# Row maxima as one VectorE scan, and VectorE's and ScalarE's order written out through the four value and gate blocks of the mLSTM layer

## The chip, the cores and the metric

The kernel runs on one core of one Trainium2 chip. The metric is the device time of one execution in microseconds (us). Before the change three runs took 598.82, 599.16 and 599.52 us, median 599.16 us.

## The reference, cut to what matters

The model has two layers over 256 positions of width 1024: an mLSTM mixer with a convolutional feed-forward network, then block-sparse attention with a second such network. The change touches the mixer alone. For each of its 4 heads (128 wide for q and k, 256 wide for v), with gates i and f:

```
u = rmsnorm(x) @ w_in ;  q, k, v, o, i, f = split(u)
b_t  = cumsum(log_sigmoid(f))                      # per head, over time
m_t  = b_t + max(0, max over s<=t of (i_s - b_s))  # "row maximum"
S_ts = (q_t . k_s) / sqrt(128) * exp(b_t - b_s + i_s - m_t)    for s <= t
h_t  = sum_s S_ts v_s / max(|sum_s S_ts|, exp(-m_t))
out  = (rmsnorm(h) * sigmoid(o)) @ w_out ;  x += out
```

The reference walks over chunks of 64 positions; the kernel does all 256 at once, which is the same sum. The running maximum over s is the part that the change computes in another way.

## The kernel before, in words

All matmuls are done on operands split in two: `hi`, a rounded copy that ScalarE makes, and `lo`, the remainder that VectorE makes; three products (hi.x, lo.x, hi.x_lo) give the needed precision. A weight arrives by DMA in units of 128x2048 numbers. `unit` takes a raw buffer (3 of them), has SyncE load it, and splits it in two pieces of 1024 columns: ScalarE `hi` (L144), VectorE `lo` (L145). There are 4 buffers for `hi` and 4 for `lo`.

**Order of the work.** TensorE runs in program order in the whole kernel (`manual_schedule`). VectorE and ScalarE run in program order from the start to `first.close()` (L579); behind that a planner places their instructions by its own estimates, and it may put a planned instruction ahead of a written one. GpSimd and SyncE are planned throughout. `behind(marks, ...)` makes the planner queue some instructions behind others. `mix(steps, items)` interleaves TensorE steps with items: each step has a cost, and an item is called ahead of the first step at which the sum of the costs so far has reached the item's time. What an item calls on VectorE and ScalarE stands, in program order, at that place too.

**The stretch that the change touches.** After the k and q projections (`kq_steps`), four blocks follow, each of 16 steps (cost 0.64, three 128x512 matmuls, L243 to L245), 8 for the first half of the rows (t=0) and 8 for the second (t=1). Block A and block B make v (units vo0, vo1 and vo2, vo3), block C and block D make the output gate o (vo4, vo5 and vo6, vo7). Within each half, steps 0 to 3 read the block's first unit and steps 4 to 7 its second. At the end of a half, `v_done` (L606 ScalarE, L607 VectorE) or `o_done` (L642, a Sigmoid on ScalarE, then L645 on VectorE for two heads, which needs those heads' `rh`) takes the result out of PSUM. Into the blocks are mixed:

- block A: `sums_f` (the cumulative sums, L477 to L481) and `maxima`: two transposes, then the running maximum of a 4x256 row set by a ladder of one copy (L487) and eight shifted maxima (L491) on VectorE, and its split in `mh`, `ml`.
- block B: four `decay` (L508 to L515), `floors`, four `scores` (L588 to L593, the last on GpSimd).
- block C: eight `head(h, t)` in the order (0,0), (0,1), (1,0), ... (3,1). A head is 3 or 6 matmuls into a `mis` PSUM buffer (L621), three small VectorE instructions for its denominator (`dn`, L625, L627, L628), a scaled copy out of PSUM (`y`, L630) and a Square with a sum (`junk`, L632) on ScalarE; with t=1 also `rh` (L635 VectorE, L636 GpSimd), which waits for the sums of both halves.
- block D: `turn(0)`, `turn(1)`: four transposes of a head's gated `y` (L653) and their split into `xb`. `project_out` follows with `turn(2)`, `turn(3)`.

There are three `mis` PSUM buffers, taken in turn. So a head's matmuls need that `y` of the head three before has been copied out.

Of the kernel before, what the change touches and what calls it, by code (L numbers as in the profile page):

```python
# [11 lines left out]
F32 = mybir.dt.float32  # L12
F32R = mybir.dt.float32r
BF16 = mybir.dt.bfloat16
AF = mybir.ActivationFunctionType
OP = mybir.AluOpType
AX = mybir.AxisListType

P = 128
D = 1024  # L20
S = 256
KD = D // P
NT = S // P
FF = 2816
KF = FF // P
MH = 4
# [19 lines left out]
C_KVNORM, C_BNORM, C_FNORM, C_HN = 0, 8, 16, 32  # L46
# [22 lines left out]

def mix(steps, items=()):  # L70

    items, now = list(items), 0.0
    for cost, step in steps:
        while items and items[0][0] <= now:
            items.pop(0)[1]()
        step()
        now += cost
    for _, item in items:
        item()
# [3 lines left out]
def yoco_kernel(ctx: ExitStack, tc: tile.TileContext, A, out):  # L83
    nc = tc.nc
# [52 lines left out]
    def unit(src, length, pieces=PIECES):  # L137
        raw = wraw.tile([P, 2048], F32, name="raw")[:, :length]
        nc.sync.dma_start(raw, src)
        hi = wsp.tile([P, 2048], F32R, name="hi")[:, :length]  # L140
        lo = wsp.tile([P, 2048], F32R, name="lo")[:, :length]
        for j in range(pieces):
            c = slice(j * length // pieces, (j + 1) * length // pieces)
            nc.scalar.activation(hi[:, c], raw[:, c], AF.Copy)  # L144
            nc.vector.tensor_tensor(lo[:, c], raw[:, c], hi[:, c].bitcast(F32), OP.subtract)  # L145
        return hi, lo

    def split(hi, lo, src, g=None):
        if g is None:
            return (nc.scalar.activation(hi, src, AF.Copy),  # L150
                    nc.vector.tensor_tensor(lo, src, hi.bitcast(F32), OP.subtract))
        return (nc.scalar.activation(hi, src, AF.Copy, scale=g),
                nc.vector.scalar_tensor_tensor(lo, src, g, hi.bitcast(F32), op0=OP.mult, op1=OP.subtract))

    def behind(marks, make):

        with ExitStack() as st:
            for m in marks:
                st.enter_context(tc.issue_after(m.ins))
            return make()  # L160

# [4 lines left out]
    setA = operand(keep, "xa", KD)  # L168
    setB = operand(keep, "xb", KD)
# [81 lines left out]
    def block_x(src, first, x, done, u=None):  # L251

        u = u or [Once(lambda j=j: unit(src[first + j], 2048)) for j in range(2)]
        return [s for t in range(NT) for s in steps_x(t, u, x, done)]
# [21 lines left out]
        else:  # L276
            feed(n, gains)

    def project_out(src, x, gains, items):

        w = [Once(lambda u=u: unit(src[u], 2048)) for u in range(4)]
        ps = [Once(acc) for n in range(KD)]

        def st(n, ks):
            return steps_w(ps[n], w[n // 2], lambda k: k * 256 + (n % 2) * P, x, ks, KD,
                           lambda p: residual(n, p, gains, False), False)

        mix([s for n in range(GROUP) for s in st(n, range(KD // 2))], items)
        mix([s for n in range(GROUP) for s in st(n, range(KD // 2, KD))])
        for n in range(GROUP, KD):  # L290
            mix(st(n, range(KD)))
# [87 lines left out]
    first = ExitStack()  # L379
# [29 lines left out]
    sel = const.tile([P, MH, P], F32, name="sel")  # L409
# [25 lines left out]
    with tc.tile_pool(name="mls", bufs=1, reuse_waits="tile") as mp, \  # L435
            tc.tile_pool(name="mlw", bufs=2, reuse_waits="tile") as mw:
        r = Rstd()

        psg = acc()
        grow, marks = [], []  # L440
        lf = mp.tile([P, NT, MH], F32, name="lf")
        gs = mp.tile([P, NT, 2 * MH], F32, name="gs")
        fc = mp.tile([P, NT, MH], F32, name="fc")
        av = mp.tile([P, NT, MH], F32, name="av")
        em = mp.tile([P, NT, MH], F32, name="em")

        mxs = [mp.tile([P, P + S], F32, name="mx0"), mp.tile([MH, P + S], F32, name="mx1")]
        mx = [t[:MH] for t in mxs]
        nc.gpsimd.memset(mxs[0], 0.0)
        nc.gpsimd.memset(mx[1][:, :P], 0.0)  # L450
        mrow = mxs[0][:, P:]
        mh = mp.tile([P, S], F32R, name="mh")
        ml = mp.tile([P, S], F32R, name="ml")
        selr = mp.tile([P, MH, P], F32R, name="selr")
# [4 lines left out]
        def gates():  # L459
            pt = mis()  # L460
            for t in range(NT):
                nc.tensor.matmul(pt[:, t * 2 * MH:(t + 1) * 2 * MH], grow[0][:, t * P:(t + 1) * P], both8,
                                 start=True, stop=True)
            for t in range(NT):
                nc.vector.scalar_tensor_tensor(gs[:, t], pt[:, t * 2 * MH:(t + 1) * 2 * MH], r.rc[:, t:t + 1],
                                               row[:, R_G:R_G + 2 * MH], op0=OP.mult, op1=OP.add)
            fg = gs[:, :, MH:]
            nc.vector.scalar_tensor_tensor(lf, fg, -1.0, fg, op0=OP.mult, op1=OP.min)
            nc.scalar.activation(lf, lf, AF.Exp)
            marks.append(nc.scalar.activation(lf, lf, AF.Ln, bias=1.0))  # L470

        def log_f():
            marks.append(nc.vector.scalar_tensor_tensor(lf, gs[:, :, MH:], 0.0, lf, op0=OP.min, op1=OP.subtract))

        def sums_f():
            pf = mis()
            nc.tensor.matmul(pf[:, :MH], tri[:, :P], lf[:, 0], start=True, stop=True)  # L477
            nc.tensor.matmul(pf[:, MH:2 * MH], tri[:, P:], lf[:, 0], start=True, stop=False)
            nc.tensor.matmul(pf[:, MH:2 * MH], tri[:, :P], lf[:, 1], start=False, stop=True)
            nc.scalar.activation(fc.rearrange("p t h -> p (t h)"), pf[:, :NT * MH], AF.Copy)  # L480
            nc.gpsimd.tensor_tensor(out=av, in0=gs[:, :, :MH], in1=fc, op=OP.subtract)  # L481

        def maxima():
            pa = mis()
            for t in range(NT):
                nc.tensor.transpose(pa[:MH, t * P:(t + 1) * P], av[:, t], ident)
            nc.vector.tensor_scalar(mx[0][:, P:], pa[:MH, :S], 0.0, None, op0=OP.max)  # L487
            src = 0
            for step in range(8):
                d = 1 << step  # L490
                nc.vector.tensor_tensor(mx[1 - src][:, P:], mx[src][:, P:],  # L491
                                        mx[src][:, P - d:P + S - d], OP.max)
                src = 1 - src

            marks[:] = split(mh[:MH], ml[:MH], mrow[:MH])
            behind(marks, lambda: nc.scalar.activation(selr, sel, AF.Copy))

        def floors():
            pc = mis()
# [28 lines left out]
        def scale(j):  # L528
            nc.vector.tensor_tensor(kq[j], kq[j], r.rB, OP.mult)
# [18 lines left out]
            squares(k, nc.vector)  # L548
        mix(kq_steps(2)[1:] + kq_steps(3))

        vo = [Once(lambda j=j: behind(marks, lambda: unit(A["w_vo"][j], 2048))) for j in range(4)]
        rawv = wraw.tile([P, 2048], F32, name="raw")
        v0 = [None, None]

# [7 lines left out]
        def between():  # L562
# [4 lines left out]
            for j in range(3):  # L567
                scale(j)
            nc.vector.tensor_tensor(v0[1][:, c], rawv[:, c], v0[0][:, c].bitcast(F32), OP.subtract)

        def then():
            log_f()
            for j in range(3, 6):
                scale(j)

        mix([s for j in range(4, 2 * MH) for s in kq_steps(j)],
            [(2.3, r.sums), (2.4, ahead), (5.4, between), (8.0, then)])
        scale(6), scale(7)
        first.close()  # L579
        vo[1]()  # L580


        PT = [[mp.tile([P, 384], F32R, name=f"PT{h}{j}") for j in range(2)] for h in range(MH)]
# [18 lines left out]
        def v_done(nb):  # L602
            def done(t, ps):
                hi, lo = (v[:, 2 * nb:2 * nb + 2, :MV] for v in V[t])
                p = ps.rearrange("p (h d) -> p h d", h=2)
                nc.scalar.activation(hi, p, AF.Copy, scale=r.rc[:, t:t + 1])  # L606
                nc.vector.scalar_tensor_tensor(lo, p, r.rc[:, t:t + 1], hi.bitcast(F32),  # L607
                                               op0=OP.mult, op1=OP.subtract)
            return done
# [48 lines left out]
        def at(t0, dt, fn, args):  # L658
            return [(t0 + dt * i, lambda a=a: fn(*a)) for i, a in enumerate(args)]

        mix(block_x(A["w_vo"], 0, setA, v_done(0), vo[:2]), [(0.6, sums_f), (2.4, maxima)])
        nc.sync.dma_start(rope, A["rope"])
        mix(block_x(A["w_vo"], 2, setA, v_done(1), vo[2:]),
            at(1.8, 0.6, decay, [(h,) for h in range(MH)]) + [(4.2, floors)]
            + at(5.1, 1.2, scores, [(h,) for h in range(MH)]))
        mix(block_x(A["w_vo"], 4, setA, o_done(0)), at(0.9, 1.05, head, [(h, t) for h in range(MH) for t in range(NT)]))
        mix(block_x(A["w_vo"], 6, setA, o_done(1)), at(2.6, 1.3, turn, [(0,), (1,)]))
        project_out(A["w_out"], setB, [(C_FNORM, setA)], at(2.8, 1.3, turn, [(2,), (3,)]))


    tab = const.tile([P, 2, NT, 2, ROT], F32, name="tab")
# [3 lines left out]
    for i in range(2):  # L675
# [3 lines left out]
        for a in range(2):  # L679
# [3 lines left out]
                op=OP.mult))  # L683
# [4 lines left out]
    with tc.tile_pool(name="att", bufs=1, reuse_waits="tile") as mp, \  # L688
# [93 lines left out]
        def it(t, fn, *a):  # L782
            return (t, lambda: fn(*a))
# [9 lines left out]
             it(4.8, turn_p, 3), it(5.2, turn, 1, 1, 1)] + [it(6.2 + 1.2 * h, logits, 4 + h) for h in range(4)])  # L793
        mix(block_x(W, 10, setA, v_done(1)),
            [it(1.0 + h, values, h) for h in range(4)] + [it(5.0 + h, turn_p, 4 + h) for h in range(4)])
        project_out(A["w_o"], setB, [(C_FNORM + KD, setA)], [it(1.0 + 0.6 * h, values, 4 + h) for h in range(4)])

    conv_ffn(1, None)

# [69 lines left out]
```

## Time and profile before

| | |
|---|---|
| median of three runs | 599.16 us |
| the profiled execution | 599.65 us, of which the span of the trace is 597.9 us |
| TensorE (PE) busy | 591.7 us, 99% of the span, 3506 matmuls |
| VectorE (DVE) busy | 484.8 us, 81% |
| ScalarE (ACT) busy | 389.8 us, 65% |
| GpSimd (POOL) busy | 159.1 us, 27% |
| granted TensorE clock | 1.00 in all of the span |
| chain that ended last | PE 96%, DVE 2%, DMA 1% |

One execution is profiled; times in the trace count from the start of its span. PE is the matmul itself, PEld the load of its weights. Matmuls are pipelined: a 128x512 matmul shows as 0.39 us long while the next one starts 0.23 us after it, so waits are read from the starts. Busy time leaves out waiting in a queue.

### The profile page before, as it was taken

Reading aid. Unit: us, or ns where it says so; the run is one execution under the profiler, and the core shown is the slowest. Engines: PE = TensorE matmul, PEld = TensorE weight load, DVE = VectorE, ACT = ScalarE, POOL = GpSimd, SP = SyncE. Lnnn points to the kernel's source line nnn. Section 1 sums busy time; section 2 is a strip of 40 time slices with the busy share of each in tenths; the row PEclk is TensorE's granted clock in tenths of the full one; section 3 lists DMA queues with packets and bytes.
Section 4 is the critical chain, followed back from the end, with each engine's and each line's share of the span. In section 5 each row is a group of like instructions: output and inputs, shape, how many; then the busy total and the mean of one; then the engine's idle time right before and its main releaser. Section 6 shows DMA issues by size and latency. Waiting matters only on the chain.

```text
span 597.9 us, 9386 instructions
## 1 busy us (share of the span) xinstructions
PE 591.7 (99%) x3506; PEld 517.7 (87%) x3506; DVE 484.8 (81%) x812; ACT 389.8 (65%) x711; POOL 159.1 (27%) x179
## 2 busy tenths in 40 slices
PE   8999999999999999999999999999999999999997
PEld 5887889998888888888888878899988888888887
DVE  5889677889999999987867777466999999998650
ACT  6748776577776776765656687555687767666430
POOL 3000411652544343311111110022454443432000
PEclk9999999999999999999999999999999999999999
DMA  8655534626454543476745533335345545336830
GB/s 296 224 208 216 206 140 142 219 115 231 148 204 158 194 168 101 167 261 221 248 175 212 203 119 130 119 141 205 142 152 199 201 159 205 108 136 212 266 109 18
DMA packets 18622, 105.80 MB, mean 177 GB/s; under 512 B 2320, under 2 KB 3856, under 8 KB 9104
## 3 DMA queue, kind: packets, MB, share of 16 engines
q1 hardware_dynamic: 18288, 104.68, 49.7%
q10 hardware_dynamic: 288, 0.52, 0.3%
q8 instruction: 27, 0.44, 0.3%
q14 instruction: 19, 0.16, 0.1%
HBM read 104.15 MB, written 1.05 MB: 176 GB/s over the span
## 4 chain that ended last, share of the span: by engine, by line
PE 96%; DVE 2%; DMA 1%; ACT 0%; issue 0%; SPq 0%; ACTq 0%; DVEq 0%
PE acc L222 39%; PE acc L226 25%; PE acc L219 10%; PE acc L243 6%; PE acc L245 6%; PE acc L244 5%; DVE lo L145 1%; PE mis L621 1%; DMA fst<-first 1%; PE mis L737 1%; PE acc L749 1%; PE mis L765 0%; PE acc L747 0%; PE acc L533 0%; PE mis L588 0%
## 5 line engine op out<-in xcount | busy, mean ns | idle before, releaser
L145 DVE TENSOR_TENSOR lo<-raw,hi 128x1024 fp32r<-128x1024 f32 (+1 forms) x210 | 238.1, 1168 | 33.5 <-ACT hi L144 33.2
L144 ACT ACTIVATE hi<-raw 128x1024 fp32r<-128x1024 f32 (+1 forms) x210 | 193.1, 968 | 46.1 <-PE acc L222 20.3
L222 PE MATMUL acc<-xb,hi 128*128 128x512 f32 x608 | 207.6, 396 | 0.0
L226 PE MATMUL acc<-xb,lo 128*128 128x256 f32 x736 | 191.7, 280 | 0.0
L226 PEld LDWEIGHTS acc<-xb,lo 128*128 128x128 f32 x736 | 138.2, 189 | 6.7
L222 PEld LDWEIGHTS acc<-xb,hi 128*128 128x128 f32 x608 | 108.7, 188 | 20.6
L222 PE MATMUL acc<-f,hi 128*128 128x512 f32 x330 | 115.0, 394 | 0.0
L308 DVE SCALAR_TENSOR_TENSOR y<-whole,par,y 128x254 f32<-128x254 f32 (+1 forms) x176 | 109.9, 639 | 5.5 <-ACT y L305 5.0
L226 PE MATMUL acc<-f,lo 128*128 128x256 f32 x352 | 96.8, 282 | 0.0
L323 POOL TENSOR_TENSOR a<-sg,y 128x256 f32<-128x256 f32 x44 | 51.8, 1176 | 96.5 <-ACT sg L321 96.5
L305 ACT ACTIVATE y<-whole,par 128x256 f32<-128x256 f32 x88 | 52.0, 593 | 32.1 <-DVE whole L264 32.1
L222 PEld LDWEIGHTS acc<-f,hi 128*128 128x128 f32 x330 | 61.1, 188 | 13.0
L226 PEld LDWEIGHTS acc<-f,lo 128*128 128x128 f32 x352 | 66.1, 188 | 1.3
L325 POOL TENSOR_TENSOR f<-a,f 128x256 fp32r<-128x256 f32 x44 | 45.1, 1026 | 43.7 <-ACT f L324 43.7
L243 PE MATMUL acc<-hi,xa 128*128 128x512 f32 x128 | 53.2, 415 | 0.0
L244 PE MATMUL acc<-lo,xa 128*128 128x512 f32 x128 | 50.1, 392 | 0.4 <-DVE lo L145 0.4
L245 PE MATMUL acc<-hi,xa 128*128 128x512 f32 x128 | 50.2, 392 | 0.0
L178 POOL TENSOR_TENSOR sqacc<-sqacc,sq 128x256 f32<-128x256 f32 x18 | 18.7, 1037 | 107.2 <-ACT sq L177 107.1
L219 PE MATMUL acc<-xb,hi 128*128 128x256 f32 x256 | 45.4, 283 | 0.0
L226 PE MATMUL acc<-xa,lo 128*128 128x256 f32 x160 | 44.6, 290 | 0.0
L219 PEld LDWEIGHTS acc<-xb,hi 128*128 128x128 f32 x256 | 39.0, 191 | 0.2
L219 PE MATMUL acc<-xa,hi 128*128 128x256 f32 x192 | 34.6, 283 | 0.0
(190 smaller groups left out, 739.1 us busy)
## 6 DMA issues: line engine op xcount, KB each, us to landing
raw<-w_up SPq DMA_DIRECT2D x44, 1024.0 KB, 4.8
raw<-w_down SPq DMA_DIRECT2D x32, 704.0 KB, 4.7
raw<-w_kqv SPq DMA_DIRECT2D x12, 1024.0 KB, 4.8
raw<-w_vo SPq DMA_DIRECT2D x8, 1024.0 KB, 4.8
raw<-w_out SPq DMA_DIRECT2D x4, 1024.0 KB, 4.8
raw<-w_o SPq DMA_DIRECT2D x4, 1024.0 KB, 4.8
raw<-w_kq SPq DMA_DIRECT2D x2, 1024.0 KB, 8.6
raw<-w_kq SPq DMA_DIRECT2D x2, 512.0 KB, 7.7
```

Source lines behind the costliest of these rows:

```text
L144: nc.scalar.activation(hi[:, c], raw[:, c], AF.Copy)
L145: nc.vector.tensor_tensor(lo[:, c], raw[:, c], hi[:, c].bitcast(F32), OP.subtract)
L219: nc.tensor.matmul(p[:, :S], hi[:, c], xs[k], start=alone[0] and k == 0 and n == 0, stop=alone[1] and last and n == 1)
L222: nc.tensor.matmul(p, hi[:, c], both[k], start=k == 0, stop=last)
L226: nc.tensor.matmul(p[:, :S], lo[:, c], xh[k], start=False, stop=False)
L243: nc.tensor.matmul(p, xh[k][:, ts], hi[:, c], start=k == 0, stop=False)
L244: nc.tensor.matmul(p, xh[k][:, ts], lo[:, c], start=False, stop=False)
L245: nc.tensor.matmul(p, xl[k][:, ts], hi[:, c], start=False, stop=k == KD - 1)
L305: nc.scalar.activation(y, u, AF.Identity, bias=b, scale=w[2])
L308: nc.vector.scalar_tensor_tensor(y[:, d:], u[:, :S - d], w[j], y[:, d:], op0=OP.mult, op1=OP.add)
L323: nc.gpsimd.tensor_tensor(out=a, in0=sg, in1=y[0], op=OP.mult)
L325: nc.gpsimd.tensor_tensor(out=al[i], in0=a, in1=ah[i].bitcast(F32), op=OP.subtract)
```

## The change

The ladder becomes one `tensor_tensor_scan` (running maximum along the row, straight from PSUM), and `av`, its input, moves from GpSimd to VectorE. `first.close()` moves behind block D, so that VectorE and ScalarE follow program order through all four blocks. The places at which units are split are written as items of `mix`, which now sorts its items by their times; `behind` and `marks` go. `project_out` is given its units; the attention layer's call makes them as before.

```
-        mxs = [mp.tile([P, P + S], F32, name="mx0"), mp.tile([MH, P + S], F32, name="mx1")]
...
+        mrow = mp.tile([P, S], F32, name="mrow")
+        zero = mp.tile([MH, S], F32, name="zero")
...
-            nc.gpsimd.tensor_tensor(out=av, in0=gs[:, :, :MH], in1=fc, op=OP.subtract)
+        def rows_a():
+            nc.vector.tensor_tensor(av, gs[:, :, :MH], fc, OP.subtract)
...
-            nc.vector.tensor_scalar(mx[0][:, P:], pa[:MH, :S], 0.0, None, op0=OP.max)
-            src = 0
-            for step in range(8):
-                d = 1 << step
-                nc.vector.tensor_tensor(mx[1 - src][:, P:], mx[src][:, P:],
-                                        mx[src][:, P - d:P + S - d], OP.max)
-                src = 1 - src
-
-            marks[:] = split(mh[:MH], ml[:MH], mrow[:MH])
-            behind(marks, lambda: nc.scalar.activation(selr, sel, AF.Copy))
+            nc.vector.tensor_tensor_scan(mrow[:MH], zero, pa[:MH, :S], 0.0, op0=OP.max, op1=OP.max)
+            split(mh[:MH], ml[:MH], mrow[:MH])
+
+        def select():
+            nc.scalar.activation(selr, sel, AF.Copy)
...
-        def then():
-            log_f()
-            for j in range(3, 6):
-                scale(j)
+            scale(3), scale(4)
 
         mix([s for j in range(4, 2 * MH) for s in kq_steps(j)],
-            [(2.3, r.sums), (2.4, ahead), (5.4, between), (8.0, then)])
-        scale(6), scale(7)
-        first.close()
-        vo[1]()
+            [(2.3, r.sums), (2.4, ahead), (5.4, between), (7.3, log_f), (8.0, vo[1])])
+        for j in range(5, 2 * MH):
+            scale(j)
...
-        mix(block_x(A["w_vo"], 0, setA, v_done(0), vo[:2]), [(0.6, sums_f), (2.4, maxima)])
+        wo = [Once(lambda u=u: unit(A["w_out"][u], 2048)) for u in range(4)]
+        mix(block_x(A["w_vo"], 0, setA, v_done(0), vo[0:2]),
+            [(1.6, sums_f), (2.6, rows_a), (4.3, maxima), (6.0, vo[2]), (7.5, vo[3]), (8.6, select)])
         nc.sync.dma_start(rope, A["rope"])
-        mix(block_x(A["w_vo"], 2, setA, v_done(1), vo[2:]),
-            at(1.8, 0.6, decay, [(h,) for h in range(MH)]) + [(4.2, floors)]
+        mix(block_x(A["w_vo"], 2, setA, v_done(1), vo[2:4]),
+            at(1.8, 0.6, decay, [(h,) for h in range(MH)]) + [(4.2, floors), (6.5, vo[4]), (9.7, vo[5])]
             + at(5.1, 1.2, scores, [(h,) for h in range(MH)]))
-        mix(block_x(A["w_vo"], 4, setA, o_done(0)), at(0.9, 1.05, head, [(h, t) for h in range(MH) for t in range(NT)]))
-        mix(block_x(A["w_vo"], 6, setA, o_done(1)), at(2.6, 1.3, turn, [(0,), (1,)]))
-        project_out(A["w_out"], setB, [(C_FNORM, setA)], at(2.8, 1.3, turn, [(2,), (3,)]))
+        mix(block_x(A["w_vo"], 4, setA, o_done(0), vo[4:6]),
+            at(0.9, 1.05, head, [(h, t) for h in range(MH) for t in range(NT)]) + [(3.4, vo[6]), (7.0, vo[7])])
+        mix(block_x(A["w_vo"], 6, setA, o_done(1), vo[6:8]),
+            [(1.0, wo[0]), (6.5, wo[1])] + at(2.6, 1.3, turn, [(0,), (1,)]))
+        first.close()
+        project_out(wo, setB, [(C_FNORM, setA)], at(2.8, 1.3, turn, [(2,), (3,)]))
```

## Rows read from the trace of the kernel before

**Rows 1.** Busy time by stretch: blocks A, B, C, D, the rest; length, then engines' busy (instructions), clock, DMA.
```profile
34.22:46.30 12.08, 12.04 (x57) 9.70 (x56) 9.94 (x22) 3.90 (x8) 0.96 (x1) 1.00 0.45 170
46.30:62.94 16.64, 15.64 (x75) 12.30 (x74) 16.64 (x25) 13.83 (x20) 1.34 (x1) 1.00 0.68 252
62.94:78.36 15.42, 15.42 (x85) 13.24 (x84) 9.41 (x30) 11.64 (x25) 5.07 (x6) 1.00 0.40 137
78.36:90.19 11.83, 11.83 (x57) 9.79 (x56) 9.11 (x19) 8.83 (x18) 1.39 (x2) 1.00 0.49 177
90.19:597.90 507.71, 504.44 (x3079) 447.49 (x3077) 416.09 (x674) 327.40 (x596) 144.30 (x141) 1.00 0.49 170
```

**Rows 2.** Timeline, TensorE: start, length, engine, line, operation, tiles, count, [idle before <-releaser].
```profile
34.68 0.40 PE L245 MATMUL acc<-hi,xa 128*128 128x512 f32 x1
35.12 0.36 PE L477 MATMUL mis<-lf,tri 128*128 128x4 f32 x2
...
46.30 0.39 PE L243 MATMUL acc<-hi,xa 128*128 128x512 f32 x1
47.05 0.50 PE L244 MATMUL acc<-lo,xa 128*128 128x512 f32 x1 [0.36 <-DVE lo L145]
...
53.64 0.40 PE L245 MATMUL acc<-hi,xa 128*128 128x512 f32 x1
54.68 0.70 PE L588 MATMUL mis<-kq,kq 128*128 128x256 f32 x2 [0.64 <-DVE E L513]
```

**Rows 3.** Timeline, ScalarE and VectorE, end of the k and q projections.
```profile
32.08 0.21 ACT L470 ACTIVATE lf<-lf 128x8 f32<-128x8 f32 x1
...
34.48 0.42 DVE L264 TENSOR_TENSOR kq<-acc,kq 128x256 f32<-128x256 f32 x1 [1.82 <-ACT kq L263]
34.82 0.16 DVE L473 SCALAR_TENSOR_TENSOR lf<-gs,lf 128x8 f32<-128x8 f32 x1
```

**Rows 4.** Timeline, ScalarE and VectorE: splits of units, a head's denominator, two heads' copies.
```profile
44.69 5.79 ACT L144 ACTIVATE hi<-raw 128x1024 fp32r<-128x1024 f32 x6
45.77 4.63 DVE L145 TENSOR_TENSOR lo<-raw,hi 128x1024 fp32r<-128x1024 f32 x4 [1.05 <-ACT hi L144]
...
63.73 2.00 ACT L144 ACTIVATE hi<-raw 128x1024 fp32r<-128x1024 f32 x2
66.51 1.96 DVE L145 TENSOR_TENSOR lo<-raw,hi 128x1024 fp32r<-128x1024 f32 x1
68.47 0.19 DVE L625 TENSOR_SCALAR dn<-mis,em 128x1 f32<-128x1 f32 x1
68.89 0.16 DVE L628 RECIPROCAL dn<-dn 128x1 f32<-128x1 f32 x1
...
73.07 0.47 ACT L630 ACTIVATE kq<-mis,dn 128x256 f32<-128x256 f32 x1
73.99 0.46 ACT L630 ACTIVATE kq<-mis,dn 128x256 f32<-128x256 f32 x1
```

**Rows 5.** Groups by line, 34 to 91 us: count | busy us, mean ns | idle before.
```profile
L491 DVE TENSOR_TENSOR mx<-mx 4x256 f32<-4x256 f32 x8 | 3.3, 411 | 0.2
L645 DVE SCALAR_TENSOR_TENSOR kq<-kq,rh,og 128x256 f32<-128x256 f32 x6 | 2.7, 483 | 2.5 <-ACT og L642 1.8 <-POOL rh L636 0.7
L642 ACT ACTIVATE og<-acc,rc 128x512 f32<-128x512 f32 x4 | 2.7, 684 | 0.8 <-PE acc L245 0.7
L642 ACT ACT_TABLE_LOAD x1 | 1.3, 1283 | 0.0
```

**Rows 6.** Timeline, TensorE: the heads (1,1), (3,0) and (3,1), and turn(0).
```profile
69.16 0.77 PEld L621 LDWEIGHTS mis<-V,PT 128*128 128x128 f32 x6 [0.24 <-ACT kq L630]
...
74.53 0.53 PE L621 MATMUL mis<-V,PT 128*128 128x258 f32 x3
...
75.59 0.88 PE L621 MATMUL mis<-V,PT 128*128 128x258 f32 x6
...
81.80 0.60 PE L653 MATMUL mis<-ident,kq 128*128 128x128 f32 x4
```

More of the change, by code (lines that the diff above doesn't have):

```diff
@@ L70, in mix @@
 def mix(steps, items=()):
-    items, now = list(items), 0.0
+    items, now = sorted(items, key=lambda i: i[0]), 0.0
     for cost, step in steps:
@@ L153, in split @@
                 nc.vector.scalar_tensor_tensor(lo, src, g, hi.bitcast(F32), op0=OP.mult, op1=OP.subtract))
[L155 to L160, printed above, removed]
     def operand(pool, name, n):
@@ L277, in residual, with project_out @@
             feed(n, gains)
-    def project_out(src, x, gains, items):
-        w = [Once(lambda u=u: unit(src[u], 2048)) for u in range(4)]
+    def project_out(w, x, gains, items):
         ps = [Once(acc) for n in range(KD)]
@@ L439, in yoco_kernel @@
         psg = acc()
-        grow, marks = [], []
+        grow = []
         lf = mp.tile([P, NT, MH], F32, name="lf")
@@ L445, in yoco_kernel @@
         em = mp.tile([P, NT, MH], F32, name="em")
-        mxs = [mp.tile([P, P + S], F32, name="mx0"), mp.tile([MH, P + S], F32, name="mx1")]
[L448 to L451, printed above, removed]
+        mrow = mp.tile([P, S], F32, name="mrow")
+        nc.gpsimd.memset(mrow, 0.0)
+        zero = mp.tile([MH, S], F32, name="zero")
+        nc.gpsimd.memset(zero, 0.0)
         mh = mp.tile([P, S], F32R, name="mh")
@@ L469, in gates @@
             nc.scalar.activation(lf, lf, AF.Exp)
-            marks.append(nc.scalar.activation(lf, lf, AF.Ln, bias=1.0))
+            nc.scalar.activation(lf, lf, AF.Ln, bias=1.0)
         def log_f():
-            marks.append(nc.vector.scalar_tensor_tensor(lf, gs[:, :, MH:], 0.0, lf, op0=OP.min, op1=OP.subtract))
+            nc.vector.scalar_tensor_tensor(lf, gs[:, :, MH:], 0.0, lf, op0=OP.min, op1=OP.subtract)
         def sums_f():
@@ L549, in yoco_kernel @@
         mix(kq_steps(2)[1:] + kq_steps(3))
-        vo = [Once(lambda j=j: behind(marks, lambda: unit(A["w_vo"][j], 2048))) for j in range(4)]
+        vo = [Once(lambda j=j: unit(A["w_vo"][j], 2048)) for j in range(8)]
         rawv = wraw.tile([P, 2048], F32, name="raw")
@@ L795, in yoco_kernel @@
             [it(1.0 + h, values, h) for h in range(4)] + [it(5.0 + h, turn_p, 4 + h) for h in range(4)])
-        project_out(A["w_o"], setB, [(C_FNORM + KD, setA)], [it(1.0 + 0.6 * h, values, 4 + h) for h in range(4)])
+        project_out([Once(lambda u=u: unit(A["w_o"][u], 2048)) for u in range(4)], setB, [(C_FNORM + KD, setA)], [it(1.0 + 0.6 * h, values, 4 + h) for h in range(4)])
     conv_ffn(1, None)
```

## The prediction

> **What bounds the kernel now.** I read the busy times first, then the stretches, then TensorE's own timeline. Behind block D nothing is to be had or lost cheaply: 504.44 of 507.71 us are matmuls at full clock, and the code there is unchanged [rows 1]. The blocks are bound by TensorE too; only in block B does it stand, with 15.64 busy of 16.64 us, while VectorE is busy for all 16.64. Where it stands, the starts tell (the next matmul follows after 0.23): 0.44 ahead of `sums_f`, which waits for `log_f`; 0.75 at the start of block B, where unit vo2's first `lo` comes late; 1.04 ahead of the first `scores`, whose PSUM buffer VectorE holds [rows 2]. That is 0.21 + 0.52 + 0.81 = 1.54 us, and with the 0.24 that head (1,1) waits [rows 6] 1.78 us: all that the change can give back.
>
> **How the written order binds.** Ahead of the old `first.close()` the two engines are already in program order, and a row shows how hard: `lf` is ready at 32.3, yet `log_f` runs at 34.82, because L264 stands ahead of it and VectorE idles 1.82 us for its input [rows 3]. The change extends this to block D. So I place every instruction of ScalarE and VectorE in program order and let each start when its engine and its inputs are there.
>
> **The parts that give.** The ladder, one L487 and eight L491 of 0.41 us [rows 5], is 3.7 us of VectorE. A scan of this size is not in the trace. It can't be under one L491, 0.41, and I see no reason for it to exceed the ladder, 3.7; I take 0.6, near the single pass over the same 4x256 numbers. [...] The scan can last 2.8 us before anybody is late: the transposes are through at about 40.1 (34.22, seven steps of 0.69, 0.67 for `sums_f`, 0.4), behind it come `mh`, a V copy and vo2's first piece, 3.4 us together, and block B wants that piece at 46.3. At the ladder's 3.7 it would cost 0.9. `av` on VectorE stands among small instructions there, between 0.15 and the 0.5 of a 128x256 one; the same cover hides it. `log_f` now stands ahead of L264 and is through at 33.6, `sums_f` comes at 36.3: 0.21 gone. vo2 is split at 42 to 45.5, vo3 by 47.5: 0.52 gone. In block B VectorE has 9 pieces, decays and scores in order of need, and the first `scores` finds its buffer: 0.81 gone. Block A to B end 1.54 earlier; block C starts at 62.94 - 1.54 = 61.4. The DMAs are issued earlier by one to two us with raw buffers that come free earlier; each unit's raw data lies there over 2 us before its split (vo6's buffer is vo3's, free at 47.5), so I cost them at nothing.
>
> **The part that takes: block C.** Its heads are TensorE items on three `mis` buffers, so head (3,0) needs `y` of (1,1) copied out, and head (3,1) that of (2,0); the trace shows this link where (1,1) waits 0.24 for `y` of (0,0) [rows 6]. What stands between on the two queues is now fixed: vo5, (0,0), (0,1), (1,0), **vo6**, (1,1), **o_done of t=0**, (2,0), (2,1), **vo7**, (3,0), (3,1), o_done of t=1. Durations [rows 4]: a `hi` piece 0.965 (5.79 for six), its `lo` starts 1.08 behind it and takes 1.16 (4.63 for four); from a head's first `dn` to its `y` 0.68 (0.42 to the last one's start, 0.16, 0.1 of hand-over); from `y` through its Square to the next thing on ScalarE 0.92.
> - vo5's `hi` begins 0.79 behind the start of block C, as before (63.73 against 62.94): 62.19. `lo` from 63.27 to 65.59. Only then may VectorE do the heads' `dn`, though (0,0) left TensorE at 63.1.
> - `y` (0,0) at 66.27, (0,1) at 67.19, its sum at 68.11, `rh`, then `y` (1,0) at 68.86, done with its Square at 69.78.
> - vo6: `hi` from 69.78, `lo` from 70.86 to 73.18. Behind it `dn` and `y` of (1,1): 73.86, out of PSUM at 74.4. TensorE is at (3,0) at 61.4 + (74.53 - 62.94 - 0.24) = 72.75 [rows 6]: **wait 1.65**.
> - ScalarE goes on: Square to 74.78, the Sigmoid's table 1.28, `og` 0.68 [rows 5]: 76.8 with the hand-over. VectorE stands for it with two L645 (0.9) ahead of `dn` of (2,0): `y` (2,0) at 78.4, out at 78.9. TensorE is at (3,1) at 74.4 + 1.06 = 75.46: **wait 3.45**. Before, the planner had put most of (2,0)'s `dn` ahead of the L645, and vo6 behind the heads.
> - `y` (2,1) at 79.3, vo7's `hi` from 80.2, `lo` to 83.6, `y` (3,0) at 84.3, (3,1) at 85.2, `og` of t=1 from 86.1 to 86.8, L645 of head 0 by 87.4. TensorE ends block C at 78.9 + 2.77 = 81.7 and is at `turn(0)` 3.44 later, 85.1 [rows 1, 6]; it starts at 87.5: **wait 2.4**. Block D ends 8.39 later, at 95.9, against 90.19.
> `turn(2)` and `turn(3)` in `project_out` find their gates ready, some 1 us ahead, and wo0 and wo1 are split by 95.
>
> **Sum.** -1.54 - 0.24 + 1.65 + 3.45 + 2.4 = +5.7 us. The profiled execution took 599.65 (span 597.9 and 1.75 around it), 0.5 over the median; it would be 605.35, and the median 599.16 + 5.7 = **604.9 us**.
>
> Bounds of this sum: GpSimd's last `PT` runs beside vo5's `lo`; one such piece took 1.96 in place of 1.16 [rows 4], and two of them put 1.6 on the chain: 606.5. Hand-overs that I have put too long by 0.1 in some ten places take 1 us off: 603.9.
>
> **The rivals.**
> 1. *The heads keep ahead* (faster). Place: the `mis` buffer of (1,1). If `y` (1,1) is out by 72.7 and `y` (2,0) by 73.8, TensorE never stands and only the gains are left: 599.16 - 1.8 = 597.4. For it: block C passes with one wait of 0.24 before, though there `y` (1,1) and (2,0) come only at 73.07 and 73.99 [rows 4] for the (3,0) and (3,1) at 74.53 and 75.59. Against it: it wants 5.1 us off the second chain, which is made of a table load, `og` and two L645 that the written order puts ahead of (2,0).
> 2. *Half of it.* If the splits come 2 us earlier than I place them (ScalarE free sooner at the end of block B), the first wait goes, and the others are 3.1 and 2.4: end of block D 93.9, 602.9; further down to 601 if `turn(0)`'s wait is smaller too.
> 3. *More.* The slowed pieces above, and a planned split of wo2 put ahead of the last `og`: 606.5 to 608.
> 4. *The order is not what I read.* If the written order is loosened by the planner, the engines fill their gaps as before, and scan and `log_f` are worth some tenths: 599.0. Against it: the 1.82 us idle [rows 3].
>
> **How the numbers follow.** The forecast 0.66 (603.2 to 606.5), rival 3 0.08, rival 2 0.10, rival 4 0.06, rival 1 0.10. Faster by over 0.2% (1.2 us, about what can be told from no change here) is rival 1, 0.10; within it rival 4, 0.06; slower the rest, 0.84. The range leaves out rivals 1 and 4 and part of 3: 600.3 to 606.9.
>
> **What would show it.** In the trace after: one scan of 0.4 to 0.8 us; no wait at the start of block B nor ahead of the first `scores`; block C beginning near 61.3. Then TensorE waiting for L630 ahead of two heads late in block C (1.7 and 3.4) and for L645 ahead of L653 (2.4); VectorE idle behind the last `dn` of (1,1) until `og`; the table load between `y` (1,1) and `y` (2,0); block D ending near 96. I am wrong if TensorE waits nowhere in block C, or if the `dn` of (2,0) run ahead of the first L645.

## The result, and the profile after

The changed kernel takes 604.76 us, the median of five runs (604.33 to 604.88); the kernel before took 599.52 us beside it (598.82 to 600.03). The ratio is 1.0087, with a 95% interval of 1.0074 to 1.0100: slower by 5.2 us. The forecast was 604.9, and +5.7 on the kernel before. The profiled execution took 604.88 us, 603.2 of it the span, so it is 5.23 over the profiled execution of before (599.65).

Windows by block after the change: the stretch, its length, then busy time and instructions of PE, PEld, DVE, ACT and POOL, the granted clock, DMA share and GB/s. Block A, B, C, D, the rest.

```profile
33.55:45.41 11.86, 11.86 (x57) 9.78 (x56) 8.25 (x13) 5.93 (x10) 0.00 (x0) 1.00 0.45 173
45.41:60.26 14.85, 14.85 (x76) 12.53 (x74) 10.20 (x19) 8.27 (x14) 2.03 (x2) 1.00 0.38 141
60.26:82.52 22.26, 17.53 (x86) 14.39 (x85) 11.48 (x31) 14.58 (x29) 4.09 (x5) 0.85 0.41 142
82.52:95.00 12.48, 12.08 (x57) 9.77 (x56) 9.08 (x20) 9.20 (x17) 0.70 (x1) 1.00 0.47 168
95.00:603.20 508.20, 504.84 (x3079) 447.60 (x3077) 417.69 (x676) 328.35 (x598) 144.14 (x141) 1.00 0.49 172
```

Against [rows 1], A takes 11.86 us in place of 12.08 (-0.22), B 14.85 in place of 16.64 (-1.79), C takes 22.26 in place of 15.42 (+6.84), D 12.48 in place of 11.83 (+0.65), the rest +0.49. Block A also begins 0.67 earlier, and 0.07 less lies outside the span: -0.22 - 1.79 + 6.84 + 0.65 + 0.49 - 0.67 - 0.07 = +5.23. So nearly all that was lost was lost in block C, and in 4.73 of its 22.26 us TensorE isn't busy.

The waits of TensorE from 33 to 100 us (released by; total, times, longest), and its timeline there: start, length, engine, line, operation, tiles, count, idle before and what ended it.

```profile
PE mis L604 <- ACT kq L613: 4.7, 2, 2.9
PE mis L636 <- DVE kq L628: 0.4, 1, 0.4
```

```profile
67.90 0.51 PE L604 MATMUL mis<-V,PT 128*128 128x258 f32 x3
...
73.68 0.62 PE L604 MATMUL mis<-V,PT 128*128 128x258 f32 x3 [1.81 <-ACT kq L613]
...
78.30 1.66 PE L604 MATMUL mis<-V,PT 128*128 128x258 f32 x6 [2.92 <-ACT kq L613]
79.76 0.63 PE L236 MATMUL acc<-hi,xa 128*128 128x512 f32 x1
80.19 0.63 PE L237 MATMUL acc<-lo,xa 128*128 128x512 f32 x1
...
86.72 0.44 PE L636 MATMUL mis<-ident,kq 128*128 128x128 f32 x2 [0.40 <-DVE kq L628]
```

The first line is head (2,0). The lines with a wait are the three places of the forecast: head (3,0) at 73.68, head (3,1) at 78.30, and at 86.72 the second half of `turn(0)`, the one that needs the gate of t=1; the waits of [rows 2] are gone. The two lines behind 78.30 show what was not forecast: 128x512 matmuls start 0.43 us apart, where in the trace of before they start 0.23 apart. The windows of block C say why (same columns as above):

```profile
60.26:71.71 11.45, 11.45 (x64) 9.78 (x62) 6.25 (x16) 7.88 (x16) 2.70 (x3) 1.00 0.54 185
71.71:73.68 1.97, 0.16 (x1) 0.00 (x0) 1.28 (x4) 0.49 (x2) 0.00 (x0) 1.00 0.24 33
73.68:74.99 1.31, 1.31 (x6) 0.94 (x6) 0.17 (x1) 1.29 (x3) 0.54 (x1) 0.78 0.54 200
74.99:78.30 3.31, 0.40 (x1) 0.00 (x0) 1.77 (x8) 1.66 (x4) 0.16 (x1) 0.50 0.52 218
78.30:81.04 2.74, 2.74 (x9) 2.45 (x10) 0.54 (x2) 2.71 (x7) 0.70 (x1) 0.50 0.00 0
81.04:82.52 1.48, 1.48 (x8) 1.22 (x7) 1.48 (x2) 0.55 (x1) 0.00 (x0) 0.94 0.00 0
```

TensorE stands 1.97 us ahead of (3,0) and 3.31 ahead of (3,1), 5.28 together. Behind the first of them the granted clock (last figure but two) falls from 1.00 to 0.78 and 0.50, and it is at 0.94 in the last window. What is left of block C's +6.84, with the 0.24 that head (1,1) no longer waits [rows 6], is 6.84 + 0.24 - 5.28 = 1.8 us. Of these, 1.70 lie behind the waits: the matmuls from head (3,0) to the end of block C take 1.31 + 2.74 + 1.48 = 5.53 us and took 1.06 + 2.77 = 3.83 before [rows 1, 6]. This is the lower clock.

The two queues behind these waits: ScalarE, then VectorE, in the columns of the timeline above. L613 is a head's `y` (L630 before), L144 a `hi` piece, L145 a `lo` piece, L608 the first `dn`, L625 `og` with its table, L628 the gate (L645 before).

```profile
69.10 1.99 ACT L144 ACTIVATE hi<-raw 128x1024 fp32r<-128x1024 f32 x2
73.16 0.47 ACT L613 ACTIVATE kq<-mis,dn 128x256 f32<-128x256 f32 x1 [2.06 <-DVE dn L611]
74.19 1.28 ACT L625 ACT_TABLE_LOAD   x1
75.48 0.69 ACT L625 ACTIVATE og<-acc,rc 128x512 f32<-128x512 f32 x1
77.78 0.47 ACT L613 ACTIVATE kq<-mis,dn 128x256 f32<-128x256 f32 x1 [1.61 <-DVE dn L611]
...
83.65 0.47 ACT L613 ACTIVATE kq<-mis,dn 128x256 f32<-128x256 f32 x1 [2.06 <-DVE dn L611]
85.48 0.67 ACT L625 ACTIVATE og<-acc,rc 128x512 f32<-128x512 f32 x1
```

```profile
39.47 0.67 DVE L480 TENSOR_TENSOR_SCAN mrow<-zero,mis 4x256 f32<-4x256 f32 x1 [2.72 <-PE mis L479]
...
70.18 2.36 DVE L145 TENSOR_TENSOR lo<-raw,hi 128x1024 fp32r<-128x1024 f32 x2 [2.09 <-ACT hi L144]
72.46 0.21 DVE L608 TENSOR_SCALAR dn<-mis,em 128x1 f32<-128x1 f32 x1
...
76.28 0.88 DVE L628 SCALAR_TENSOR_TENSOR kq<-kq,rh,og 128x256 f32<-128x256 f32 x2 [1.91 <-ACT og L625]
77.08 0.21 DVE L608 TENSOR_SCALAR dn<-mis,em 128x1 f32<-128x1 f32 x1
```

To see here: `y` of (1,1) comes at 73.16 because its `dn` (72.46) stands behind vo6's two `lo` pieces, which stand behind its two `hi` pieces. `y` of (2,0) comes at 77.78 because its `dn` (77.08) stands behind the two L628, which stand idle for 1.91 us until table and `og` are through. In both cases ScalarE in turn idles for VectorE (2.06 and 1.61): each engine waits in its own queue for the other. The chain that ended last, followed back, doesn't touch TensorE from 54.98 us (block B's first `scores`) to 86.72: it runs on these two queues alone. The forecast had these `y` at 73.86, 78.4, 84.3 and `og` at 86.1; they are 0.6 to 0.7 earlier, as the start of block A is. The matmuls of (2,0), at 67.90, were through (68.41) long before TensorE began to wait for (3,0) at 71.71, and yet its `dn` (77.08) did not pass the L628 (76.28) that VectorE idled for.

### The profile page after: what moved, and what is told of

It reads as the page before. It is cut to its first block, busy times and chain, and to the rows that moved or that the text cites. A ratio compares the mean times of both kernels' runs of the same rounds, so it can differ in the third digit from the quotient of the medians.

```text
span 603.2 us, 9371 instructions
## 1 busy us (share of the span) xinstructions
PE 592.1 (98%) x3506; PEld 517.8 (86%) x3506; DVE 481.6 (80%) x805; ACT 390.4 (65%) x711; POOL 157.0 (26%) x178
## 3 DMA queue, kind: packets, MB, share of 16 engines
HBM read 104.15 MB, written 1.05 MB: 174 GB/s over the span
## 4 chain that ended last, share of the span: by engine, by line
PE 93%; DVE 3%; ACT 3%; DMA 1%; issue 0%; SPq 0%; ACTq 0%; DVEq 0%
PE acc L215 38%; PE acc L219 24%; PE acc L212 10%; PE acc L236 5%; PE acc L238 5%; PE acc L237 5%; DVE lo L145 2%; DMA hT<-xT 1%; ACT hi L144 1%; ACT kq L613 1%; PE mis L725 1%; PE acc L737 1%; ACT junk L615 1%; PE mis L753 0%; PE acc L735 0%
## 5 line engine op out<-in xcount | busy, mean ns | idle before, releaser
L145 DVE TENSOR_TENSOR lo<-raw,hi 128x1024 fp32r<-128x1024 f32 (+1 forms) x210 | 236.7, 1163 | 34.0 <-ACT hi L144 33.9
L144 ACT ACTIVATE hi<-raw 128x1024 fp32r<-128x1024 f32 (+1 forms) x210 | 193.0, 968 | 41.6 <-PE acc L215 20.2
```

## The experiments

Each was timed beside the kernel before on the same chip; ratios are to that one. Line numbers shift a little from kernel to kernel.

**1. Is it the buffers or the order?** The heads (3,0) and (3,1) get a PSUM buffer of the projection's kind, so that neither has to wait for a `mis` buffer.

```
-            pn = mis()[:, :MV + 2]
+            pn = (acc if h == MH - 1 else mis)()[:, :MV + 2]
```

> The changed kernel with one edit: the matmuls of heads (3,0) and (3,1) go into buffers of the accumulator pool, so TensorE no longer needs the copies of (1,1) and (2,0). Theory Q (the written order of ScalarE and VectorE sets the end of block D): both waits for L613 vanish, TensorE runs into block D some 5 us earlier and stands there for the same late work, vo7's pieces (about 3 us) and turn(0) (about 4 us); block D ends at 95 as before and the time stays at 604.8 +-0.5. Rival P (three mis buffers are too few, and that is all): the two waits, 4.7 to 5.3 us, are gone and nothing takes their place: 599.5 to 600.

606.19 us, ratio 1.0119 (1.0106 to 1.0133): no gain, which rules out rival P, but also 1.4 more than the 604.8 expected. Both waits for `y` are gone, and the time is not. TensorE's waits from 60 to 100 us, the second half of `turn(0)` in its timeline, and two windows from there on:

```profile
PE mis L636 <- DVE kq L628: 3.8, 1, 3.8
PE acc L236 <- ACT hi L144: 2.3, 1, 2.3
PE acc L237 <- DVE lo L145: 0.8, 1, 0.8
```

```profile
86.62 0.69 PE L636 MATMUL mis<-ident,kq 128*128 128x128 f32 x2 [3.81 <-DVE kq L628]
```

```profile
86.62:91.00 4.38, 4.38 (x15) 3.60 (x16) 3.58 (x5) 2.49 (x5) 0.00 (x0) 0.57 0.23 65
91.00:96.65 5.65, 5.65 (x26) 4.64 (x25) 4.76 (x7) 4.99 (x7) 0.00 (x0) 1.00 0.41 168
```

That half starts at 86.62, against 86.72 after the change: the two queues run on as before, and TensorE only waits elsewhere, for the pieces of vo6 and vo7 and for the gate. The buffers carry the wait, they don't make it. Block D ends 1.65 later (96.65) because the 3.81 now lie ahead of the last matmuls of the stretch, and the lower clock behind them (0.57) falls where no later wait can take it up: from the second half of `turn(0)` to the end of block D pass 10.03 us, against 8.28 after the change.

**2. The first gate later.** `o_done` for t=0 is called at 9.0, behind the last head.

```
...
+                if nb == 0 and t == 0 and not later:
+                    later.append(lambda: done(t, ps))
+                    return
...
-            at(0.9, 1.05, head, [(h, t) for h in range(MH) for t in range(NT)]) + [(3.4, vo[6]), (7.0, vo[7])])
+            at(0.9, 1.05, head, [(h, t) for h in range(MH) for t in range(NT)]) + [(3.4, vo[6]), (7.0, vo[7]), (9.0, lambda: later[0]())])
```

> The changed kernel with o_done of t=0 of block C (table load, og, two L628) called at 9.0, behind head (3,1), in place of ahead of (2,0). Theory Q, instruction by instruction: the wait at (3,0) stays at 2.0, that at (3,1) falls from 3.3 to about 0.8, turn(0) then waits about 4.4 since vo7 and the gates still come late; block D ends 0.6 earlier, 604.2. A rival R (the second wait, behind the Sigmoid's table and the gates, is the one that costs): 2.6 us less, 602.2.

605.13 us, ratio 1.0103 (1.0088 to 1.0117): 0.9 more than the 604.2 expected. The wait ahead of (3,1) shrinks from 3.31 to 0.68, and the one at `turn(0)` grows from 0.54 to 2.28 us (4.4 expected):

```profile
PE mis L604 <- ACT kq L613: 2.3, 2, 1.8
PE mis L641 <- DVE kq L633: 2.1, 1, 2.1
```

So taking table, `og` and gate out from between the heads moves the wait along the same chain, as the theory of the queue said, and rival R's gain of 2.6 us is out. What the theory missed is the end: counted from the start of block A, `turn(0)` starts at 51.96 in place of 53.17 for its second half after the change, 1.2 earlier, and yet block D ends 62.14 behind that start in place of 61.45. From `turn(0)` to the end of block D pass 10.18 us, against 8.39 before: behind the 2.28 us of wait the 128x512 matmuls start 0.43 apart again (86.62, 87.05, 87.47, 87.90), and nothing later takes that up.

**3. The units later.** vo6 and vo7 behind the heads.

```
-            at(0.9, 1.05, head, [(h, t) for h in range(MH) for t in range(NT)]) + [(3.4, vo[6]), (7.0, vo[7])])
+            at(0.9, 1.05, head, [(h, t) for h in range(MH) for t in range(NT)]) + [(9.0, vo[6]), (9.8, vo[7])])
```

> The changed kernel with vo6 and vo7 split at 9.0 and 9.8, behind the heads, in place of 3.4 and 7.0 among them. Theory Q: no wait at (3,0), about 1.4 at (3,1), then block D waits about 3.4 for vo6 and 0.4 for vo7 and not for turn(0); block D ends 2.6 earlier, 602.2. If the splits among the heads were all of the cost: 599 or below. If order R above holds: within 0.7 of 604.8.

603.41 us, ratio 1.0069 (1.0057 to 1.0082): 1.2 us more than the 602.2 expected. The chain is shorter, but not by what was expected: block D ends 60.37 behind the start of block A in place of 61.45, 1.08 earlier and not 2.6. The waits came about as expected, 1.50 us at head (3,1) and 2.20 + 1.03 for vo6's two kinds of pieces at the start of block D (3.4 expected). What was not expected is that the clock falls behind them:

```profile
77.00:81.00 4.00, 1.20 (x5) 0.46 (x4) 1.68 (x4) 3.94 (x10) 0.70 (x1) 1.00 0.00 0
81.00:85.00 4.00, 4.00 (x12) 3.09 (x12) 4.00 (x6) 3.78 (x4) 0.00 (x0) 0.57 0.50 164
```

Block D takes 16.76 us; without its 3.23 of waits that is 13.53, against 11.83 before, 1.7 more.

**4. The written order only to the end of block B.** `first.close()` goes ahead of block C.

```
+        first.close()
         mix(block_x(A["w_vo"], 4, setA, o_done(0), vo[4:6]),
...
-        first.close()
```

> The changed kernel with first.close() ahead of block C: the written order ends with block B, and the planner places ScalarE and VectorE in blocks C and D as before. Theory Q: blocks A and B keep their gain (block C begins 2.0 us after block A earlier than before the change), and C and D take about what they took before the change, 27.3 us together: 599.5 - 1.8 = 597.7, at least 6 us under the changed kernel. A rival (the gain in A and B is the planner's loss in C, since the units come in other buffers and order): 599 to 600.

599.62 us, ratio 1.0015 (1.0006 to 1.0024): a miss for the theory, which had the gain of A and B kept, and inside the rival's 599 to 600. The gain is there (block C starts 26.71 us behind block A, as after the change), and is then lost: block C takes 18.1 us, and from the start of block A to the end of D pass 56.67 us, 0.7 more than the 55.97 of before. ScalarE in block C, and TensorE's waits from 60 to 100 us:

```profile
61.35 5.78 ACT L144 ACTIVATE hi<-raw 128x1024 fp32r<-128x1024 f32 x6
67.04 0.45 ACT L613 ACTIVATE kq<-mis,dn 128x256 f32<-128x256 f32 x1
```

```profile
PE mis L604 <- ACT kq L613: 2.1, 2, 1.1
```

The planner puts vo5, vo6 and vo7 in one row of six pieces ahead of the first `y`. TensorE waits for it twice, 1.1 and 1.3 us by the starts. An earlier start of block C is worth nothing while the units are placed so. Still, of the 5.2 us that the change costs, 4.3 go with this one line (the ratios 1.0087 and 1.0015 differ by 0.0072 of 599 us): the loss is made by this written order in C and D.

**5. The scan alone**, in the kernel before, with `av` left on GpSimd.

```
...
-            nc.vector.tensor_scalar(mx[0][:, P:], pa[:MH, :S], 0.0, None, op0=OP.max)
...
+            nc.vector.tensor_tensor_scan(mrow[:MH], zero, pa[:MH, :S], 0.0, op0=OP.max, op1=OP.max)
```

> The kernel before with one edit: the ladder becomes the scan; its written order, planner, unit places and av on GpSimd stay. Theory Q: the scan does not bind by itself; it frees 3 us of VectorE ahead of block B, so that the 0.52 at the start of block B goes and perhaps the 0.81 ahead of the first scores, and in block C the planner's order, which e4 showed to stand about 2 us for PSUM buffers once it begins earlier, takes part of that back: 598.0 to 599.3, 0 to 1.3 us under the kernel before. A rival (the scan is what gains, the written order what loses): the 2 us of blocks A and B and no loss, 597.0.

598.40 us against 599.06, ratio 0.9985 (0.9976 to 0.9994): the one version that is faster than the kernel before, by 0.7 us. The scan in its timeline of VectorE:

```profile
37.78 0.67 DVE L486 TENSOR_TENSOR_SCAN mrow<-zero,mis 4x256 f32<-4x256 f32 x1
```

It frees 3.0 us of VectorE (3.7 less 0.67), of which the path gets 0.85: from the start of block A to the end of block D 55.12 us pass, against 55.97. The other small moves of the change (`log_f`, `av`) were not run by themselves.

**6. The change without the scan**: the ladder comes back, the order stays.

```
...
-            nc.vector.tensor_tensor_scan(mrow[:MH], zero, pa[:MH, :S], 0.0, op0=OP.max, op1=OP.max)
+            nc.vector.tensor_scalar(mx[0][:, P:], pa[:MH, :S], 0.0, None, op0=OP.max)
...
```

> The changed kernel with the ladder back in place of the scan, all else as changed. Theory Q: the ladder takes some 3.4 us from 39.5 and vo2's first lo then comes 0.5 after block B wants it, selr 0.3 after the first decay: block D ends 0.9 later, 605.7. If the cover of 2.8 us that the prediction gave the scan were larger than that: 604.8, no change; if the ladder were on the chain from the start: 607.5.

606.20 us, ratio 1.0124 (1.0109 to 1.0140); 605.7 was expected. The ladder on VectorE, and block B's second matmul on TensorE:

```profile
39.09 0.41 DVE L481 TENSOR_SCALAR mx<-mis 4x256 f32<-4x256 f32 x1 [2.71 <-PE mis L480]
39.54 3.54 DVE L485 TENSOR_TENSOR mx<-mx 4x256 f32<-4x256 f32 x8
```

```profile
46.42 0.50 PE L237 MATMUL acc<-lo,xa 128*128 128x512 f32 x1 [0.76 <-DVE lo L145]
```

The forecast said that the ladder would be late by 0.9 in this order: block B's second matmul starts 1.26 behind its first (45.16) in place of 0.23, a wait of 1.03. With smaller stands behind it block B takes 16.28 us, 1.43 more than after the change. So the scan is needed for the gain in block B. Over the four blocks the ladder costs more than the 0.9 expected: 63.43 us from the start of block A to the end of D, against 61.45, +1.98. The total shows less, since here block A started 0.39 earlier and the part behind block D took 0.39 less.

**7. The clock by itself.** Filler matmuls on a constant, whose result nobody reads, stand where TensorE would wait: 8 ahead of (3,0), 15 ahead of (3,1), 10 ahead of `turn(0)`.

```
...
+        def fill(n):
+            for j in range(n):
+                nc.tensor.matmul(pfill(), warm[:, :P], warm, start=True, stop=True)
...
+            + [(7.15, lambda: fill(8)), (8.2, lambda: fill(15))])
...
+            [(1.0, wo[0]), (2.55, lambda: fill(10)), (6.5, wo[1])] + at(2.6, 1.3, turn, [(0,), (1,)]))
```

> The changed kernel with matmuls on a constant, into a spare accumulator that nobody reads, put where TensorE stands: 8 ahead of head (3,0), 15 ahead of (3,1), 10 ahead of turn(0), of 0.22 us each. They keep TensorE busy and change nothing else. Theory Q: the granted clock stays at 1.00, block C ends some 1.8 us earlier, turn(0) still starts at 86.7 because its gate comes then; block D ends at 95 and the time stays at 604.8 +-0.5. Rival K (part of the price is the clock that falls after the waits, 1.8 us in block C): 603.0.

604.59 us, ratio 1.0094 (1.0081 to 1.0108). Two windows from block C's start to block D's end, `turn(0)` in TensorE's timeline, and the gates of t=1 in VectorE's:

```profile
60.07:82.00 21.93, 21.73 (x112) 16.08 (x112) 11.15 (x31) 14.59 (x29) 4.09 (x5) 1.00 0.40 144
82.00:95.01 13.01, 12.94 (x62) 9.84 (x62) 9.61 (x20) 9.38 (x18) 0.69 (x1) 1.00 0.44 162
```

```profile
83.94 2.11 PE L649 MATMUL acc<-warm 128*128 128x512 bf16 x9
...
86.57 0.60 PE L636 MATMUL mis<-ident,kq 128*128 128x128 f32 x4
```

```profile
86.00 0.88 DVE L628 SCALAR_TENSOR_TENSOR kq<-kq,rh,og 128x256 f32<-128x256 f32 x2 [0.41 <-ACT og L625]
```

The clock stays at 1.00, and block C ends at 80.99, 20.92 us behind its start in place of 22.26. TensorE would be early at `turn(0)` and fills that time with matmuls for nobody. The second half of `turn(0)` could not have started before 86.54: after the change it starts 0.54 behind the first gate of t=1 (86.18 and 86.72), and here that gate starts at 86.00. So the fillers cost it at most some 0.2 us, and block D ends at 95.01, as after the change (95.00). The lower clock in block C cost nothing: it is taken out of the wait that follows. Slower matmuls behind the last wait do cost, 1.7 to 1.8 us in experiments 1 to 3.

**8. The same written order, with the pieces in another place.** vo4 and vo5 are split earlier in block B, vo6 at the start of C, vo7 at its end, and `rh` stands directly ahead of `og` and the gates (not shown below).

```
...
-            at(1.8, 0.6, decay, [(h,) for h in range(MH)]) + [(4.2, floors), (6.5, vo[4]), (9.7, vo[5])]
+            at(1.8, 0.6, decay, [(h,) for h in range(MH)]) + [(4.2, floors), (1.3, vo[4]), (4.5, vo[5])]
...
-            at(0.9, 1.05, head, [(h, t) for h in range(MH) for t in range(NT)]) + [(3.4, vo[6]), (7.0, vo[7])])
+            at(0.9, 1.05, head, [(h, t) for h in range(MH) for t in range(NT)]) + [(0.1, vo[6]), (10.0, vo[7])])
```

> The changed kernel with another written order: vo4 split at 1.3 and vo5 at 4.5 in block B, vo6 at 0.1 ahead of the heads, vo7 at 10.0 behind them, and L618 with its GpSimd power taken out of the heads and put at the head of o_done of t=0. Theory Q, instruction by instruction: waits of 0.2 in block B, 0.3 at head (3,1) and 0.4 at vo7 are all that is left, the clock does not fall, block D ends at 88.2 to 88.8 in place of 95.0: 597.9 to 598.5 where the changed kernel takes 604.8, 1 to 2 us under the kernel before. If a written order as such loses against the planner: 600 or more.

599.11 us, ratio 1.0005 (0.9996 to 1.0014). The time from block A to the end of D falls from 61.45 to 55.19, as expected, and the 5.2 us are gone; the total misses its 597.9 to 598.5, because `turn(2)` in `project_out` now waits, and behind block D pass 508.89 us in place of 507.71:

```profile
93.02 0.44 PE L637 MATMUL mis<-ident,kq 128*128 128x128 f32 x2 [0.60 <-DVE kq L629]
```

The moves were made together; which of them gives how much was not tried.

**9 and 10. Behind the blocks.** Experiment 9 splits vo7's two pieces apart and queues wo2 and wo3 behind the last gate; experiment 10 queues them behind `turn(3)`'s split instead. Both start from experiment 8.

```
...
+        wo += [Once(lambda u=u: behind_last(lambda: unit(A["w_out"][u], 2048))) for u in (2, 3)]
...
+            at(0.9, 1.05, head, [(h, t) for h in range(MH) for t in range(NT)]) + [(0.1, vo[6]), (9.1, lambda: vo7(0)), (10.0, lambda: vo7(1))])
```

> The order of e8 with two further edits: the two pieces of vo7 are split at 9.1 and 10.0 in place of both at 10.0, and the units wo2 and wo3, which the planner had put ahead of the last og and its gates, are queued behind these. Theory Q: vo7's wait of 0.2 and the wait of turn(2) in project_out (0.7, with 0.3 behind it) go, that at head (3,1) stays at 0.6: 1.0 to 1.4 us under e8, a ratio of 0.997 to 0.999 to the kernel before. If the wait of turn(2) had another cause, the ratio stays at 1.0005.

> The order of e9 with wo2 and wo3 queued behind the split of turn(3) in project_out, as they ran in the kernel before, in place of behind the last gate. In e9 block D ended 0.4 earlier than in e8, and the planner's placing of wo2 and wo3 ahead of turn(2)'s split gave it back: TensorE stood 1.7 in project_out. Theory Q: that wait goes and nothing takes its place, 1.5 to 2 us under e9, a ratio of 0.996 to 0.9985 to the kernel before. If the loss behind block D moves on with the units: 0.999 to 1.0005.

599.11 us, ratio 1.0006 (0.9997 to 1.0015), and 600.97 us, ratio 1.0034 (1.0021 to 1.0048): both miss. Block A to D takes 54.80 and 54.81 us, 0.4 less again. In experiment 9 the planner then puts both units in a row ahead of the last heads' `xb`, on ScalarE

```profile
88.87 3.89 ACT L144 ACTIVATE hi<-raw 128x1024 fp32r<-128x1024 f32 x4
92.66 0.46 ACT L152 ACTIVATE xb<-mis,par 128x256 fp32r<-128x256 f32 x1
```

and TensorE waits 1.05, 0.38 and 0.29 us in `project_out`. In experiment 10 that is gone, and a wait stands in the feed-forward network (waits from 60 to 130 us):

```profile
PE mis L184 <- DVE sqacc L171: 2.1, 1, 2.1
PE mis L604 <- ACT kq L613: 0.4, 1, 0.4
```

What the written part gives, the planned part behind it gives back, each time in another place. Whether an order written out over `project_out` and the feed-forward network would keep it was not tried and stays open.

## Why the prediction was right, step by step

- **Block A and B, -1.54.** Right: no wait at the start of block B nor ahead of the first `scores`. Measured -2.01: 0.22 in block A (forecast 0.21), 1.79 in B (forecast 1.33). Of the 0.46 more in B, 0.34 lie in three gaps of some 0.1, two behind the two waits of before and one ahead of the transposes of `floors`, which I had not counted. Experiment 5 shows what the scan alone gives over the four blocks: 0.85.
- **The scan, 0.6 by a bound of 0.41 to 3.7.** Measured 0.67 (VectorE's timeline above), 0.26 over one pass of the ladder, 0.41. That a scan can't be shorter than one such pass was my estimate from the ladder's rows, and no row shows the 0.8 up to which I looked for it in the trace. One size was measured, so no run here shows what sets the 0.67.
- **Head (3,0), +1.65, and head (3,1), +3.45.** Measured 1.97 and 3.31 by the starts, released by the `y` that the forecast named, behind vo6's pieces and behind table, `og` and gates. The start of block C was forecast at 61.4 and came at 60.26: 0.67 by the earlier start of block A, 0.47 by the larger gain. I had hung the chain on that start, with vo5's `hi` 0.79 behind it; it came 1.14 behind it (61.40), since the chain lies on the two queues from block B on. So the larger gain hardly moved the chain; it made the wait at (3,0) longer.
- **`turn(0)`, +2.4: the mis-sized term.** Measured 0.54. TensorE was to reach it at 85.1, 2.4 us ahead of the gate, and reached it only 0.54 ahead of the release, mostly since the lower clock had cost it some 1.7 us in block C (5.53 us of matmuls in place of 3.83), which stands nowhere in the sum. The two errors cancel, and not by luck: experiment 7 takes the clock loss away, and block D ends no earlier (95.01). That I left out a clock that can fall was harmless only because a wait came behind it: in experiments 1 to 3 the same omission made me miss by 0.9 to 1.4 us. The instant of `turn(0)`'s second half is set by the chain of ScalarE and VectorE, which I had placed to 0.1 of the truth once block A's start is taken off (87.5 - 0.67 = 86.83; measured 86.72).
- **Sum, +5.7.** From the start of block A to the end of D 55.97 became 61.45, +5.48, near the +5.7. The rest adds +0.49, which I forecast at nothing, and the start-up takes 0.67 off, with 0.07 less outside the span: +5.23. Most of the 0.49 lies in `project_out`: `turn(2)` and `turn(3)` were to find all ready, but the planner put wo2's pieces ahead of the last `og` (ScalarE, the two lines below) and wo3's ahead of the splits into `xb`, and TensorE stands three times there, for 0.07 to 0.3. The start-up seems no part of the change: block A starts at 33.15 in experiment 5, which has the old order there, and at 33.04 to 34.08 in the experiments that have the new one. That these two nearly cancel is luck, and so is the agreement of 604.76 with 604.9: the difference was 5.2 in place of 5.7, and the kernel before took 599.52 beside it in place of 599.16.

```profile
92.28 3.90 ACT L144 ACTIVATE hi<-raw 128x1024 fp32r<-128x1024 f32 x4
96.07 0.69 ACT L625 ACTIVATE og<-acc,rc 128x512 f32<-128x512 f32 x1
```

- **Rivals.** That the heads keep ahead (597.4) and that the planner loosens the order (599.0) fall by the waits in the trace. Half of it (602.9) had its splits 2 us earlier; they were 0.7 earlier, and so was everything else. Of *more* (606.5 to 608) half came about: wo2 did go ahead of the last `og`, but cost less than the 0.49; vo5's two pieces were not slowed (62.48 to 64.84, 1.18 each). Experiment 1 shuts out a reading that I had not priced, that PSUM buffers are the bound.

What experiment 4 corrects is my picture of the kernel before: its planner does not simply fill gaps well. With the units of this change it puts six pieces ahead of the first `y`, so that an early start of block C is of no use. Experiment 8 shows the other half: the written order costs 5 us by where four units and `rh` stand in it, not because it is written.

## What to carry to other kernels

When the order of two engines is written out, place every instruction on each queue and let it start when its queue and its input are there; the instant at which the last queue delivers sets the end. Waits, buffers and clock ahead of that instant only shared out the same time here (block D ended at 95.01 with the fillers of experiment 7, at 95.00 without); matmuls that slowed behind it had to be paid for (1.7 to 1.8 us, experiments 1 to 3). A long piece, or one that waited for another engine's slow result, held up everything short behind it (2.36 us of `lo` pieces and 1.91 us of idling for `og`, each ahead of a `dn` of 0.21). Moving one of them may only move the wait (experiment 2); what gave the 5.2 us back was to place all of the units anew (experiment 8). And look behind the written stretch as well: where a planner goes on, a gain can be given back in its first free choice.

## What the runs showed of the hardware

The granted clock fell from 1.00 to 0.50 around two waits of 1.97 and 3.31 us with 1.31 us of matmuls between them, with 128x512 matmuls then starting 0.43 apart in place of 0.23. It was 0.57 over the 4.38 us behind a wait of 3.81 by the trace with two shorter ones ahead of it (experiment 1), and 0.57 from 81 to 85 us, behind waits of 2.20 and 1.03 (experiment 3). Behind the wait of 2.28 in experiment 2 the matmuls started 0.43 apart too. The clock stayed at 1.00 through the two waits of 1.1 and 1.3 us of experiment 4. Filler matmuls kept it at 1.00 (experiment 7) without any gain in time. Where matmuls slowed so behind the last wait, it cost 1.7 to 1.8 us (experiments 1 to 3). A running maximum along 4x256 numbers took 0.67 us as one scan, where nine plain instructions of 0.41 took 3.7.
